# Heads of 64: where the probabilities of an attention are divided by their row sums

## The chip, the cores and the metric

The kernel runs on one core of a Trainium2 chip, in one launch. The metric is the time on the device in microseconds. The kernel before has a median of 2105.86 us over three runs (2103.87 to 2106.68).

## The reference, cut to what matters

A two-layer encoder over 512 positions of width 1024 in float32. Each layer has a feed-forward block, a mixer, a cross-attention to 256 memory positions and a second feed-forward block. In both mixers there are attentions with heads of 64: eight heads in layer 0 (dsa_attention, with a choice of keys by an index), sixteen in layer 1 (chunk_band_attention). All of them end in the same two steps, a softmax over the keys and a product with the values:

```
logits = jnp.einsum('bqhd,bkhd->bhqk', qc, kc).astype(jnp.float32) * dh ** -0.5 + bias[None]
logits = jnp.where(valid, logits, -jnp.inf)
p = jax.nn.softmax(logits, axis=-1).astype(vc.dtype)
return jnp.einsum('bhqk,bkhd->bqhd', p, vc)
```

## The kernel before

TensorE multiplies float32 numbers as pairs of a high and a low part (names that end in h and l: wh and wl, pz0h and pz0l). So one product is three matmuls, and each operand needs a cast on ScalarE (the high part) and a subtraction on VectorE or GpSimd (the low part, such as wl of a weight, L159).

The heads of 64 are computed by attend64, six calls with two passes over j each: four passes in layer 0 ("A" heads), eight in layer 1 ("C" heads). A pass takes a pair of heads, z=0 and z=1. Its steps, in the order in which TensorE does them:

- make_q and make_k turn the queries and keys (L745 and L764: four transposes each), and VectorE and ScalarE split them in two parts (qz, kz);
- close finishes the head z=1 of the pass before;
- the logits of z=0 (L791), then those of z=1. Queries lie on the partitions. A block of 128 queries has its own tile of 128 to 512 keys, e0 to e3. VectorE adds the bias and takes the row maximum in one operation (L804), ScalarE takes the exponential and adds up the row sums rs (L805);
- finish for z=0: ten transposes of 128x128 (L816, transpose_p) bring the keys to the partitions, in the order of e0, e1, e2, e3, and then the further blocks of e1, e2 and e3; ScalarE and VectorE split them (pz0h, pz0l and so on, L819 and L820); eight matmuls (L843) give the output, with queries along the row. The sum of its two parts (L847 on ScalarE, L848 on VectorE) goes to the rows of this head in the pair's tile o (its name in rows is x);
- finish for z=1 is left to the next pass (self.pend).

The output is divided by the row sums only at the end of a pair. rc holds the reciprocals, one column for each block (L869). GpSimd spreads a column over 64 columns (rb, L835), TensorE transposes rb in four pieces (L852), and VectorE multiplies o with the result (L853).

On TensorE the program order is the order written down. Between the steps of the attention stand pieces of a projection, six matmuls of 512 columns each, which weave (L79) pulls: an attention yields a number (its pace), and weave takes pieces, each worth 1300, until the number is used up. So a pace of 600 gives one piece, 1950 two, 2600 two, 3250 three, 4550 four and 0 none. In A the four paces are 3900, 600, 1950 and 0 (after make_k, after the logits of either head, after the transposes, after the PV product); in C they were 4550, 600, 2600 and 600. The orders of VectorE, ScalarE, GpSimd and the DMA queue are set by a scheduler.

In the last passes of A and C the woven pieces belong to the projection of the memory's keys and values (L1083; its tiles are ml, wl, vp and the row sums ss) and to the output projection (L636, whose results are added at L649).

Of the kernel before, what the change touches and what calls it, by code (L numbers as in the profile page):

```python
# [11 lines left out]
F32 = mybir.dt.float32  # L12
# [3 lines left out]
OP = mybir.AluOpType  # L16
# [3 lines left out]
P = 128  # L20
S = 512
# [4 lines left out]
QB = S // P  # L26
# [8 lines left out]

A_QK = 3900
A_S = 600
A_PT = 1950
A_PV = 0
B_QK = 7800  # L40
B_S = 2000
B_PT = 2600
B_PV = 600
C_QK = 4550
C_S = 600
C_PT = 2600
C_PV = 600
I_1 = 1500
# [58 lines left out]
class Encoder:  # L107
# [722 lines left out]
    def attend64(self, qk, vp, vbase, base, gcol, biasname, o_tiles, mp, masks=None):  # L830

        nc = self.nc

        def finish(es, rc, h, z, o, rb):
            nc.gpsimd.tensor_copy(rb.rearrange("p (i c) -> p i c", c=P)[:, :, z * 64:z * 64 + 64],  # L835
                                  rc.unsqueeze(2).to_broadcast([P, QB, 64]))
            self.transpose_p(es)
            yield self.pace[2]
            p = self.bank("pb")
            c = 0  # L840
            for jb, pz, src, q0, n in self.PV:
                for t in self.pz[pz]:
                    nc.tensor.matmul(p[:, q0:q0 + n], vp[jb][:, h * P:(h + 1) * P], t[:, src:src + n],  # L843
                                     start=c == 0, stop=c == 7)
                    c += 1
            tmp = mp.tile([64, S], F32, name="ot", tag="ot", bufs=1)
            nc.scalar.copy(tmp, p[64:128, :])  # L847
            nc.vector.tensor_add(o[z * 64:z * 64 + 64, :], p[0:64, :], tmp)  # L848
            if z == 1:
                p = self.bank("pb")  # L850
                for i in range(QB):
                    nc.tensor.transpose(p[:, i * P:(i + 1) * P], rb[:, i * P:(i + 1) * P], self.ident)  # L852
                nc.vector.tensor_mul(o, o, p)  # L853
                self.done(o)
            yield self.pace[3]

        for j in (0, 1):
            q = self.make_q(qk, j * P)
            k = self.make_k(qk, 256 + j * P, gcol)
            yield self.pace[0]  # L860
            yield from self.close()
            rb = mp.tile([P, S], F32, name="rb", tag="rb", bufs=1)
            sts = []
            for z in (0, 1):
                h = 2 * (base + j) + z
                bias = self.bias_tile(biasname, h, mp)
                es, rs = self.softmax_exp(self.logits(q, k, z, masks), bias, mp)
                rc = self.small.tile([P, 4], F32, name="rc", tag="rc", bufs=4)
                nc.vector.reciprocal(rc, rs)  # L869
                sts.append(finish(es, rc, h - vbase, z, o_tiles[j], rb))  # L870
                yield self.pace[1]
            yield from sts[0]
            self.pend = sts[1]

# [458 lines left out]
    def mixer0(self):  # L1333
        pre, I = "l0_", self.I
        with ExitStack() as ctx:
            self.qkbufs, self.vbufs, self.ebufs = 10, 8, 2
            mp = self.open_mixer(ctx, pre)
            xs, acc = self.xs, self.acc
            os = self.park_x()
            w = I[pre + "w_in"]  # L1340
            nlam = self.lam()
            ga = self.gain_col(pre + "a_q_norm", pre + "a_k_norm", 64 ** -0.5)
            gb = self.gain_col(pre + "b_q_norm", pre + "b_k_norm", 64 ** -0.5)
            sub = self.small.tile([P, 1], F32, name="subg", tag="gcol", bufs=6)
            self.nc.vector.tensor_scalar(sub, self.col(pre + "b_subln"), 1.0 - LAMBDA_INIT, None, op0=OP.mult)
            ready = []
            self.pace = (A_QK, A_S, A_PT, A_PV)

            def gemm():
                self.wshare = WS[0]  # L1350
                ik, iq = [], []
                yield from self.index_gemm(ik, I["l0_w_ikw"], 72, xs)
                for j in range(4):
                    b = []
                    yield from self.index_gemm(b, I["l0_w_iq"][j], P, xs)
                    iq += self.raw(b, mp)
                    if j == 0:
                        v, r = self.var_rstd(acc)
                        ready.append((iq, ik[0], v, r))
                b = []  # L1360
                yield from self.gemm_nat(b, w[0], xs, WS[1])
                bqk = self.heads(b, v, mp)
                b = []
                yield from self.gemm_nat(b, w[1], xs, WS[2])
                bv = self.values(b, r, P, mp)
                ready.append((bqk, bv))
                b = []
                yield from self.gemm_nat(b, w[2], xs, WS[3])
                bqk = self.heads(b, v, mp)
                ready.append((bqk, bv))  # L1370
                b = []
                yield from self.gemm_nat(b, w[3], xs, WS[4])
                aqk = self.heads(b, v, mp)
                b = []
                yield from self.gemm_nat(b, w[4], xs, WS[5])
                av = self.values(b, r, 64, mp)
                ready.append((aqk, av))
                b = []
                yield from self.gemm_nat(b, w[5], xs, WS[6])
                aqk = self.heads(b, v, mp)  # L1380
                ready.append((aqk, av))
                self.wshare = WS[7]
                yield from self.mem_kv(pre, mp)
                yield from self.mix_out(I[pre + "w_out"], list(range(KB)), os, mp)

            def att():
                sc, ik = {}, []
                yield from self.wait(ready, 0)
                iq, p, v, r = ready[0]
                yield from self.index_keys(ik, p, v, r, mp)  # L1390
                yield from self.index_scores(sc, iq, *ik, mp)
                masks = {}
                top = self.index_top(masks, sc, mp)
                yield from self.along(self.wait(ready, 1), top, 1)
                yield from self.along(iter(B_N1), top, TOP_A)
                yield from self.along(self.attend_diff(*ready[1], 0, gb, "bias0", os[0:2], nlam, sub, mp), top, TOP_A)
                yield from self.wait(ready, 2)
                yield B_N2
                yield from self.along(self.attend_diff(*ready[2], 2, gb, "bias0", os[2:4], nlam, sub, mp), top, TOP_B)
                for _ in top:  # L1400
                    pass
                yield from self.wait(ready, 3)
                yield from self.attend64(*ready[3], 0, 0, ga, "bias0", os[4:6], mp, masks)
                yield from self.wait(ready, 4)
                yield from self.attend64(*ready[4], 0, 2, ga, "bias0", os[6:8], mp, masks)
                yield from self.unfinished()

            self.weave(gemm(), att())
            self.xattn(pre, mp)

    def mixer1(self):
        pre, I = "l1_", self.I
        with ExitStack() as ctx:
            self.qkbufs, self.vbufs, self.ebufs = 10, 8, 2
            mp = self.open_mixer(ctx, pre)
# [2 lines left out]
            w = I[pre + "w_in"]  # L1418
            g = self.gain_col(pre + "c_q_norm", pre + "c_k_norm", 64 ** -0.5)
            ready = []  # L1420
            self.pace = (C_QK, C_S, C_PT, C_PV)

            def gemm():
                v = None
# [134 lines left out]
```

## Time and profile before

| what | before |
|---|---|
| median of the runs | 2105.86 us |
| the profiled execution | 2105.58 us |
| its span, first to last instruction | 2103.8 us |
| TensorE busy | 2076.7 us (99%) |
| VectorE busy | 1567.4 us (75%) |
| ScalarE busy | 1135.7 us (54%) |
| GpSimd busy | 363.3 us (17%) |
| granted clock of TensorE | 1.00 throughout |

Busy shares are averages over the whole span. What a step of the attention is worth has to be read in its own stretch: the A pairs lie from about 560 to 655 us, the C pairs from about 1465 to 1680 us. The chain of work that ended last is followed back from the last instruction; where it runs through TensorE without a break, every microsecond on TensorE is one of the kernel.

### The profile page before, as it was taken

The page shows a single profiled execution, that of the slowest core. Times are in us where ns is not written, and L with a number is a line of the kernel's source. Part 1 is how long each engine was busy: PE and PEld are TensorE (multiplying, and loading weights), DVE is VectorE, ACT ScalarE, POOL GpSimd, SP SyncE. Part 2 cuts the span into 40 slices and gives each one's busy share as a digit, 9 for nine tenths or more (in the row PEclk, how much of TensorE's full clock was granted, in tenths as well). Part 3 has the DMA queues.
Part 4 walks back from the last instruction along what each step waited for, and adds up shares of the span by engine and source line. Part 5 has one row for each costly group of instructions (what it writes and reads, how often), then busy time and mean ns, then how long its engine had stood idle before and what let it go on. Part 6 is the DMA issues. An engine that isn't in the chain of part 4 may idle for free.

```text
span 2103.8 us, 32523 instructions
## 1 busy us (share of the span) xinstructions
PE 2076.7 (99%) x12834; PEld 1851.0 (88%) x12834; DVE 1567.4 (75%) x2246; ACT 1135.7 (54%) x1701; POOL 363.3 (17%) x319
## 2 busy tenths in 40 slices
PE   8999999999999999999999999999999999999999
PEld 7989897888788889998989899988888888989997
DVE  8858677699677697685889677684668688958676
ACT  6635344556685565362556254344778566626442
POOL 1101003345421210000020000013453022000000
PEclk9999999999999999999999999999999999999999
DMA  7737535222232176473356366344224225737632
GB/s 225 210 116 193 143 103 162 96 86 80 91 126 69 52 208 165 139 190 116 102 167 182 118 178 174 98 123 150 91 81 131 91 71 150 192 110 190 161 98 93
DMA packets 86122, 279.65 MB, mean 133 GB/s; under 512 B 9681, under 2 KB 12881, under 8 KB 85969
## 3 DMA queue, kind: packets, MB, share of 16 engines
q1 hardware_dynamic: 74448, 235.62, 34.1%
q0 software_dynamic: 11520, 41.95, 11.4%
q8 instruction: 101, 1.65, 0.3%
q14 instruction: 53, 0.43, 0.1%
HBM read 271.24 MB, written 6.29 MB: 132 GB/s over the span
## 4 chain that ended last, share of the span: by engine, by line
PE 87%; DVE 8%; ACT 2%; issue 2%; POOL 1%; DMA 1%; SPq 0%; DVEq 0%; ACTq 0%; POOLq 0%
PE ps_pa L447 26%; PE ps_pb L447 10%; PE ps_pa L583 10%; PE ps_pa L685 10%; PE ps_pb L583 10%; PE ps_pa L636 4%; PE ps_pa L319 3%; PE ps_pb L791 2%; PE ps_pa L1233 1%; PE ps_pb L843 1%; PE ps_pa L1083 1%; PE ps_pb L816 1%; PE ps_pb L636 1%; DVE wl L159 1%; PE ps_pa L1002 1%
## 5 line engine op out<-in xcount | busy, mean ns | idle before, releaser
L157 ACT ACTIVATE wh<-wf 128x1024 fp32r<-128x1024 f32 (+2 forms) x211 | 215.4, 1022 | 347.9 <-PE ps_pa L583 121.0
L159 DVE TENSOR_TENSOR wl<-wf,wh 128x1024 fp32r<-128x1024 f32 (+2 forms) x169 | 199.7, 1185 | 33.4 <-ACT wh L157 31.2
L425 ACT ACTIVATE wh<-s 128x1024 fp32r<-128x1024 f32 x108 | 114.4, 1059 | 105.5 <-PE ps_pb L447 35.0
L426 DVE TENSOR_TENSOR wl<-s,wh 128x1024 fp32r<-128x1024 f32 x108 | 132.5, 1227 | 51.3 <-ACT wh L425 51.1
L425 ACT ACTIVATE wh<-wf 128x1024 fp32r<-128x1024 f32 x84 | 88.9, 1058 | 110.2 <-PE ps_pa L447 36.7
L504 POOL DMA_DIRECT2D s<-l_ffn_wq x40 | 35.5, 887 | 525.8 <-ACT s L503 525.8
L159 POOL TENSOR_TENSOR wl<-wf,wh 128x1024 fp32r<-128x1024 f32 x42 | 101.4, 2415 | 138.1 <-ACT wh L157 136.2
L685 PE MATMUL ps_pa<-wh,xh 128*128 128x512 f32 x384 | 122.0, 399 | 0.1
L685 PE MATMUL ps_pa<-wh,xl 128*128 128x512 f32 x384 | 119.0, 391 | 0.0
L685 PE MATMUL ps_pa<-wl,xh 128*128 128x512 f32 x384 | 118.6, 390 | 0.0
L477 POOL DMA_DIRECT2D s<-l_ffn_wq x40 | 35.6, 889 | 456.6 <-DMA s<-l_ffn_wq 321.4
L426 DVE TENSOR_TENSOR wl<-wf,wh 128x1024 fp32r<-128x1024 f32 x84 | 102.5, 1220 | 8.8 <-ACT wh L425 5.9
L593 DVE TENSOR_TENSOR dn<-ps_pa,R 128x512 f32<-128x512 f32 x48 | 33.1, 689 | 89.2 <-PE ps_pa L583 88.9
L224 POOL TENSOR_TENSOR acc<-acc,sq 128x512 f32<-128x512 f32 (+1 forms) x37 | 54.1, 1462 | 246.4 <-ACT sq L223 245.2
L583 PE MATMUL ps_pb<-hh,wl 128*128 128x512 f32 x352 | 96.2, 392 | 0.0
L583 PE MATMUL ps_pb<-hh,wh 128*128 128x512 f32 x352 | 96.2, 391 | 0.0
L583 PE MATMUL ps_pb<-hl,wh 128*128 128x512 f32 x352 | 96.1, 391 | 0.0
L583 PE MATMUL ps_pa<-hh,wl 128*128 128x512 f32 x328 | 89.4, 392 | 0.0
L583 PE MATMUL ps_pa<-hl,wh 128*128 128x512 f32 x328 | 89.3, 391 | 0.0
L583 PE MATMUL ps_pa<-hh,wh 128*128 128x512 f32 x328 | 89.3, 391 | 0.0
L593 DVE TENSOR_TENSOR dn<-ps_pb,R 128x512 f32<-128x512 f32 x48 | 33.0, 688 | 73.4 <-PE ps_pb L583 72.9
L685 PEld LDWEIGHTS ps_pa<-wl,xh 128*128 128x128 f32 x384 | 72.1, 188 | 15.8
(377 smaller groups left out, 5938.4 us busy)
## 6 DMA issues: line engine op xcount, KB each, us to landing
wf<-l_ffn_wq SPq DMA_DIRECT2D x120, 512.0 KB, 3.6
s<-l_ffn_wq SPq DMA_DIRECT2D x80, 512.0 KB, 4.5
s<-l_ffn_wq POOLq DMA_DIRECT2D x80, 512.0 KB, 6.7
wf<-l_ffn_wd SPq DMA_DIRECT2D x64, 512.0 KB, 3.9
wf<-l_w_in SPq DMA_DIRECT2D x48, 512.0 KB, 3.3
wf<-l_ffn_wd SPq DMA_DIRECT2D x32, 384.0 KB, 3.1
wf<-l_mem_wkv SPq DMA_DIRECT2D x16, 512.0 KB, 3.3
wf<-l_w_out SPq DMA_DIRECT2D x16, 512.0 KB, 3.3
```

Source lines behind the costliest of these rows:

```text
L157: self.leading = nc.scalar.activation(wh[:, sl], w[:, sl], AF.Copy)
L159: eng.tensor_sub(wl[:, sl], w[:, sl], wh.bitcast(F32)[:, sl])
L224: self.summed = (eng or nc.gpsimd).tensor_add(acc[:, :n], acc[:, :n], sq[:, :n])
L319: nc.tensor.matmul(p, w[a][:, k * P:(k + 1) * P], xs[k][c], start=k == order[0] and a == c == 0, stop=k == order[-1] and a == 1)
L425: self.leading = nc.scalar.activation(h, t, AF.Copy)
L426: self.parted = nc.vector.tensor_sub(l, t, h.bitcast(F32))
L447: self.nc.tensor.matmul(bank[:, sl], w[a][:, o:o + P], xs[k][b], start=first and z == a == b == k == 0, stop=z == a == 1 and k == KB // 2 - 1,
L583: self.nc.tensor.matmul(bank, w[a][:, j * P:(j + 1) * P], h, start=j == a == e == 0, stop=j == nb - 1 and (a, e) == ops[-1])
L593: nc.vector.tensor_mul(t, bank, f.R)
L636: nc.tensor.matmul(banks[dd], a[:, o:o + P], parts(k)[b], start=k == first and a is wh and b == 0, stop=k == last and a is wl)
L685: nc.tensor.matmul(banks[i], xs[k][a][:, i * P:(i + 1) * P], w[b][:, kk * 512:kk * 512 + 512], start=k == a == b == 0, stop=k == KB - 1 an ...
L791: nc.tensor.matmul(bank[:, o:o + n], a, b[:, :n], start=c == 0, stop=c == len(ops) - 1)
```

## The change

It divides the probabilities instead of the outputs. For each block of queries VectorE now takes the reciprocal of the row sums (128x1) and multiplies the block's tile e in place, before the transposes: 96 reciprocals and 96 scalings, 24 each of 128, 256, 384 and 512 columns. The tile rb, its copies on GpSimd, its transposes and the last multiplication are gone. The pace after the logits now may differ between the two heads: in C the one after make_k falls from 4550 to 3250 and the one after the logits of z=1 rises from 600 to 1950; in A both stay.

```
-C_QK = 4550
+C_QK = 3250
 C_S = 600
+C_SS = 1950
...
-        def finish(es, rc, h, z, o, rb):
-            nc.gpsimd.tensor_copy(rb.rearrange("p (i c) -> p i c", c=P)[:, :, z * 64:z * 64 + 64],
-                                  rc.unsqueeze(2).to_broadcast([P, QB, 64]))
+        def finish(es, h, z, o):
             self.transpose_p(es)
...
             if z == 1:
-                p = self.bank("pb")
-                for i in range(QB):
-                    nc.tensor.transpose(p[:, i * P:(i + 1) * P], rb[:, i * P:(i + 1) * P], self.ident)
-                nc.vector.tensor_mul(o, o, p)
                 self.done(o)
             yield self.pace[3]
...
-            rb = mp.tile([P, S], F32, name="rb", tag="rb", bufs=1)
...
                 rc = self.small.tile([P, 4], F32, name="rc", tag="rc", bufs=4)
-                nc.vector.reciprocal(rc, rs)
-                sts.append(finish(es, rc, h - vbase, z, o_tiles[j], rb))
-                yield self.pace[1]
+                for i in range(QB):
+                    nc.vector.reciprocal(rc[:, i:i + 1], rs[:, i:i + 1])
+                    nc.vector.tensor_scalar(es[i], es[i], rc[:, i:i + 1], None, op0=OP.mult)
+                sts.append(finish(es, h - vbase, z, o_tiles[j]))
+                yield self.pace[1][z]
...
-            self.pace = (C_QK, C_S, C_PT, C_PV)
+            self.pace = (C_QK, (C_S, C_SS), C_PT, C_PV)
```

TensorE, fourth C pair, where the PV product of the head z=1 of the third pair ends (L843) and the logits of z=0 (L791) follow; before:

```order
L843 MATMUL ps_pb<-pz2h,vp 128x256
L843 MATMUL ps_pb<-pz2l,vp 128x256
L852 MATMUL ps_pb<-ident,rb 128x128 x4
L685 MATMUL ps_pa<-wh,xh 128x512 x2
L685 MATMUL ps_pa<-wh,xl 128x512 x2
L685 MATMUL ps_pa<-wl,xh 128x512 x2
L791 MATMUL ps_pb<-kz0h,qz_14184 128x256
L791 MATMUL ps_pb<-kz0l,qz_14184 128x256
```

and in the changed kernel (its line numbers differ a little):

```order
L845 MATMUL ps_pb<-pz2h,vp 128x256
L845 MATMUL ps_pb<-pz2l,vp 128x256
L687 MATMUL ps_pa<-wh,xh 128x512 x2
L687 MATMUL ps_pa<-wh,xl 128x512 x2
L687 MATMUL ps_pa<-wl,xh 128x512 x2
L793 MATMUL ps_pb<-kz0h,qz_14204 128x256
L793 MATMUL ps_pb<-kz0l,qz_14204 128x256
```

Only the four transposes of rb are gone; the woven piece of six matmuls stays. In A no piece stands there. Next, TensorE in the same pair, from the end of the logits of z=1 to the transposes of z=0; before:

```order
L791 MATMUL ps_pb<-kz1h,qz_14185 128x512
L791 MATMUL ps_pb<-kz1l,qz_14185 128x512
L685 MATMUL ps_pa<-wh,xh 128x512 x2
L685 MATMUL ps_pa<-wh,xl 128x512 x2
L685 MATMUL ps_pa<-wl,xh 128x512 x2
L816 MATMUL ps_pb<-ident,e_15426 128x128
L816 MATMUL ps_pb<-ident,e_15429 128x128
L816 MATMUL ps_pb<-ident,e_15432 128x128
L816 MATMUL ps_pb<-ident,e_15435 128x128
```

and in the changed kernel:

```order
L793 MATMUL ps_pb<-kz1h,qz_14205 128x512
L793 MATMUL ps_pb<-kz1l,qz_14205 128x512
L687 MATMUL ps_pa<-wh,xh 128x512 x2
L687 MATMUL ps_pa<-wh,xl 128x512 x2
L687 MATMUL ps_pa<-wl,xh 128x512 x2
L687 MATMUL ps_pa<-wh,xh 128x512 x2
L687 MATMUL ps_pa<-wh,xl 128x512 x2
L687 MATMUL ps_pa<-wl,xh 128x512 x2
L818 MATMUL ps_pb<-ident,e_15448 128x128
L818 MATMUL ps_pb<-ident,e_15451 128x128
L818 MATMUL ps_pb<-ident,e_15454 128x128
L818 MATMUL ps_pb<-ident,e_15457 128x128
```

Two pieces stand there instead of one; the second comes from the four between make_k and close. The fourth transpose reads the longest tile, e3. The last place is VectorE in the third A pair, from the maxima of z=1 on (ISA rows, the second of each two stores the maximum); before:

```order
L804 ISA e_6276,m<-ps_pb,bias 128x128
L804 ISA m 128x1
L804 ISA e_6279,m<-ps_pb,bias 128x256
L804 ISA m 128x1
L869 RECIPROCAL rc<-rs 128x4
L804 ISA e_6282,m<-ps_pb,bias 128x384
L804 ISA m 128x1
L804 ISA e_6285,m<-ps_pb,bias 128x512
L804 ISA m 128x1
L649 TENSOR_TENSOR x<-ps_pa,xr 128x512 x2
```

and in the changed kernel, where e_6252 and e_6255 are the tiles e2 and e3 of z=0, and e_6292 to e_6301 those of z=1:

```order
L806 ISA e_6292,m<-ps_pb,bias 128x128
L806 ISA m 128x1
L806 ISA e_6295,m<-ps_pb,bias 128x256
L806 ISA m 128x1
L865 RECIPROCAL rc<-rs 128x1
L866 TENSOR_SCALAR e_6252<-e_6252,rc 128x384
L806 ISA e_6298,m<-ps_pb,bias 128x384
L806 ISA m 128x1
L806 ISA e_6301,m<-ps_pb,bias 128x512
L806 ISA m 128x1
L866 TENSOR_SCALAR e_6255<-e_6255,rc 128x512
L865 RECIPROCAL rc<-rs 128x1
```

The scaling of e3 of z=0 stands behind all four maxima of z=1. It does so in each of the twelve pairs, and in the pairs C6 and C7 of layer 1 a wl (L161) and, in C7, a vp (L1093) and a row sum (L698) stand ahead of it as well.

## Rows read from the trace of the kernel before

**Rows 1.** Page: busy time by engine; chain that ended last, by engine.

```profile
PE 2076.7 (99%) x12834; PEld 1851.0 (88%) x12834; DVE 1567.4 (75%) x2246; ACT 1135.7 (54%) x1701; POOL 363.3 (17%) x319
...
PE 87%; DVE 8%; ACT 2%; issue 2%; POOL 1%; DMA 1%; SPq 0%; DVEq 0%; ACTq 0%; POOLq 0%
```

**Rows 2.** Waits of TensorE: total us, times, longest us.

```profile
PE ps_pb L816 <- DVE qz L755: 2.5, 2, 2.1
```

**Rows 3.** Chain that ended last, pair C3: start us, length us, what.

```profile
1520.39 0.44 PE ps_pb L852 x4
1520.82 1.39 PE ps_pa L685 x6
...
1527.56 1.09 PE ps_pb L816 x10
```

**Rows 4.** Lines L852 and L853: ns of one, min/median/max; first and last start.

```profile
L852 PE MATMUL ps_pb<-ident,rb x48: 270/272/273, 590.3 to 1672.7; 128*128 128x128 f32 x48
...
L853 DVE TENSOR_TENSOR x<-x,ps_pb x12: 679/686/689, 592.4 to 1674.0; 128x512 f32<-128x512 f32 x12
```

**Rows 5.** Line L970, a scaling elsewhere in the kernel: ns of one.

```profile
L970 DVE TENSOR_SCALAR sc<-rl,coef x3: 353/420/485, 385.5 to 386.5; 128x256 f32<-128x256 f32 x1, 128x384 f32<-128x384 f32 x1, 128x512 f32<-128x512 f32 x1
```

**Rows 6.** Timeline of VectorE in C3, end of the maxima of z=1: start, us.

```profile
1526.53 0.17 DVE L869 RECIPROCAL rc<-rs 128x4 f32<-128x4 f32 x1
1526.62 0.66 DVE L804 CUSTOM_DVE_ANT_0 e<-ps_pb,bias 128x512 f32<-128x512 f32 x1
1527.21 0.08 DVE L804 DVE_READ_ACCUMULATOR2_ANT m<- 128x1 f32 x1
```

**Rows 7.** Chain that ended last, pairs A2 and A3.

```profile
597.45 1.09 PE ps_pb L816 x10
...
607.60 1.15 PE ps_pb L816 x10
...
623.67 1.29 PE ps_pb L843 x8
```

**Rows 8.** Timeline of VectorE in A2 (first two rows) and A3.

```profile
591.12 0.68 DVE L848 TENSOR_TENSOR x<-ps_pb,ot 64x512 f32<-64x512 f32 x1 [1.08 <-ACT ot L847]
...
596.70 0.09 DVE L804 DVE_READ_ACCUMULATOR2_ANT m<- 128x1 f32 x1
...
622.57 0.55 DVE L820 TENSOR_TENSOR pz2l<-ps_pb,pz2h 128x384 fp32r<-128x384 f32 x1
```

**Rows 9.** Timelines of VectorE (two rows) and GpSimd in A1.

```profile
571.05 0.49 DVE L1079 SCALAR_TENSOR_TENSOR ml<-mem,cols,mh 128x256 fp32r<-128x256 f32 x1 [0.54 <-ACT mh L1077]
...
573.17 0.08 DVE L804 DVE_READ_ACCUMULATOR2_ANT m<- 128x1 f32 x1
...
573.40 2.39 POOL L159 TENSOR_TENSOR wl<-wf,wh 128x1024 fp32r<-128x1024 f32 x1
```

**Rows 10.** Timelines of GpSimd and VectorE at three places in layer 1.

```profile
1494.65 1.64 POOL L244 TENSOR_TENSOR f<-ss,mhalf 128x8 f32<-128x8 f32 x1
1495.19 0.23 DVE L699 TENSOR_SCALAR ss<-ss,epsv 128x8 f32<-128x8 f32 x1
...
1531.85 2.40 POOL L159 TENSOR_TENSOR wl<-wf,wh 128x1024 fp32r<-128x1024 f32 x1
1532.80 1.48 DVE L699 TENSOR_SCALAR ss<-ss,epsv 128x8 f32<-128x8 f32 x1
...
1577.76 2.41 POOL L159 TENSOR_TENSOR wl<-wf,wh 128x1024 fp32r<-128x1024 f32 x1 [5.72 <-ACT wh L157]
1579.27 1.44 DVE L1308 TENSOR_TENSOR ol<-x,oh 128x512 fp32r<-128x512 f32 x1
```

**Rows 11.** Two stretches: length; busy us of PE, PEld, DVE, ACT, POOL; clock.

```profile
1465.00:1600.00 135.00, 134.39 (x716) 114.78 (x715) 88.06 (x195) 99.05 (x206) 58.00 (x51) 1.00 0.26 84
1602.80:1637.00 34.20, 33.46 (x178) 27.51 (x177) 31.52 (x72) 29.65 (x64) 9.14 (x14) 1.00 0.49 159
```

More of the change, by code (lines that the diff above doesn't have):

```diff
@@ L37 @@
 A_S = 600
+A_SS = 600
 A_PT = 1950
@@ L1346, in mixer0 @@
             ready = []
-            self.pace = (A_QK, A_S, A_PT, A_PV)
+            self.pace = (A_QK, (A_S, A_SS), A_PT, A_PV)
             def gemm():
```

## Prediction

> **What bounds the kernel now.** I read the page first. TensorE is busy 2076.7 us of the 2103.8 us span and the chain that ended last runs through it for 87%; VectorE comes second with 1567.4 us [rows 1]. Then the waits of TensorE: over the whole program its longest in the attention is 2.5 us in two pieces, at the transposes of the probabilities [rows 2]. So around the change TensorE has next to no slack: work taken off it counts in full, and so does each new wait of it. The question is whether VectorE, which gets the new work, delivers in time.
>
> I call the four pairs of heads of layer 0 A1 to A4 and the eight of layer 1 C1 to C8; each is one pass of the loop over j, with the heads z=0 and z=1.
>
> **What is removed.** Twelve groups of four transposes. A group is one piece of 0.44 us of the chain [rows 3]; its line has 48 of 272 ns each [rows 4], which overlap, so the chain's piece is the price: 12 x 0.44 = 5.3 us. With them go 12 products of 0.69 us on VectorE [rows 4] and the copies on GpSimd, which is busy for 17% [rows 1].
>
> **What is added.** Per head four scalings in place, of 128, 256, 384 and 512 columns. The nearest row (L970) has 0.35, 0.42 and 0.485 us for 256, 384 and 512 columns [rows 5]; the step of 0.07 puts 128 columns at 0.29. On VectorE an operation starts some 0.08 us before the one ahead ends: the reciprocal of 128x4 lasts 0.17 and the next starts 0.09 after it [rows 6]. So the four take about 0.21 + 0.27 + 0.34 + 0.40 = 1.2 us, the removed product 0.6. The three further reciprocals take 0.09 each (one of a single column has no row: between 0.03 and 0.09). A head costs VectorE some 1.5 us more, a pair 2 x 1.5 - 0.6 = 2.4 us more.
>
> **What is moved.** In each C pair a piece of six matmuls, 1.39 us [rows 3], goes from ahead of the z=1 transposes of the pair before (C1: from ahead of the logits of z=0) to behind the logits of z=1. It costs nothing by itself, since TensorE runs the same pieces, and gives the probabilities of z=0 1.39 us more before their transposes. Those of z=1 lose as much and keep some 10 us (in A2 the transposes of z=0 start at 597.45, those of z=1 at 607.60 [rows 7]): nothing. In A nothing moves.
>
> **Where VectorE is late.** The order of instructions puts the scaling of the longest block of z=0 (e3) behind the four maximum operations of z=1 in every pair. These wait for the logits of z=1, and the fourth of the ten transposes needs e3. The ten take 1.09 us [rows 7], so the fourth starts 0.33 us into them (3 of 10).
>
> *A2 to A4*, by A2: TensorE loses 0.44 us, so the transposes of z=0 would start at 597.45 - 0.44 = 597.01 and need e3 at 597.34. VectorE began the addition of L848 at 591.12 and ended the last maximum of z=1 at 596.79, with little idle time between [rows 8]. It sheds 0.60 there (the product) and gets three scalings (0.82) and 0.27 of reciprocals, then the scaling of e3 (0.48): 597.76. TensorE waits 0.4 us in each of the three, 0 to 0.7. In A3 more comes: pz2l ended at 623.12 [rows 8], 1.35 us ahead of its first reader, the sixth of the eight matmuls that start at 623.67 [rows 7]. All the additions of the pair, some 2.3 us, now stand ahead of it: 0.6, 0 to 1.0.
>
> *A1* has no pair ahead, so nothing is shed. The last maximum ended at 573.25; with 1.1 us more, of which 0.54 fills idle time [rows 9], and the scaling, e3 is ready at 574.3, 0.2 us late by the same reckoning. But GpSimd runs L159 from 573.40 to 575.79 there [rows 9], and that operation has held VectorE: L699, 0.23 us at 1495.19, took 1.48 us from 1532.80 to 1534.28 while GpSimd ran L159 until 1534.25, and ol took 1.44 us under another L159 [rows 10]. Held so, e3 comes 1.7 us late. Between 0.2 and 1.8 I take 1.2, since by the rows GpSimd starts first.
>
> *C1 to C4*, by C3: the transposes of z=0 now start at 1527.56 - 0.44 + 1.39 = 1528.51 [rows 3] and need e3 at 1528.84. The last maximum of z=1 ended at 1527.29 [rows 6]; logits come 0.44 earlier, 1.1 us are added ahead of it and the scaling behind it: 1528.4. So 0.4 us are spare: no wait, 0.1 each for the spread, 0 to 0.3. *C5* has an L159 of GpSimd over its scalings [rows 10]: 0.4, 0 to 1.1. *C8* has a further wl ahead of e3: 0.3, 0 to 0.6.
>
> *C6 and C7* lie where the keys and values of the memory are projected, and there VectorE is nearly full: 31.52 us busy of the 34.20 from 1602.80 to 1637.00 [rows 11]. They bring 2.4 us (C6) and 0.9 (C7 up to its e3): 34.8 us of work in a stretch that TensorE would now do in 34.2 - 0.9 = 33.3. The excess is 1.5 us if VectorE never idles and 4.2 if it keeps its 2.7 us of idle time. In C7 the scaling of e3 also stands behind a wl, a vp and a row sum. I take 3.0.
>
> **The sum**: -5.3 + 1.2 (A1) + 1.2 (A2 to A4) + 0.6 (pz2l in A3) + 0.4 (C1 to C4) + 0.4 (C5) + 3.0 (C6, C7) + 0.3 (C8) = +1.8 us. The profiled execution took 2105.58 us (1.78 outside its span); the median of the runs, 2105.86, is 0.3 above it. From the profiled one: 2107.4 us. With all lower ends it is -5.3 + 1.7 = -3.6, or 2102.0; with all upper ends -5.3 + 1.8 + 2.1 + 1.0 + 1.2 + 1.1 + 4.2 + 0.6 = +6.7, or 2112.3. A change of under 0.2% (4.2 us) can hardly be told from none in this kernel, and most of this lies within it.
>
> **Rivals.** *All of it hides* (0.24). VectorE is idle for a quarter of the span, the first additions of a pair may find idle time that I counted as busy, and ScalarE may deliver its exponentials earlier. Then the 5.3 us remain: 2100.3. For it, the waits of all twelve pairs must stay under 1.1 us together; the 92% of C6 and C7 [rows 11] speak against it.
>
> *GpSimd holds the scalings* (0.18; this one ends slower). In C GpSimd is busy 58 of 135 us [rows 11]. If in each of C1 to C5 one scaling of z=0 is held over an L244 of 1.64 us [rows 10], 1.24 remain after what is spare: 5 x 1.24 - 0.8 (counted above) + 0.6 (A1 at its upper end) = +6.0 on the forecast, 2113.4 us. It decides from about 2.9 us upwards, two to three pairs held. Against it: L699 took its 0.23 us at 1495.19 in the middle of an L244 [rows 10]. The Trainium skill (SBUF — State Buffer, section Who interferes with whom) states that such a VectorE operation and any GpSimd operation exclude each other for the whole instruction, whoever starts first. By that rule L244 holds too; the rows on L159 agree with it and the one on L244 does not, if only for eight columns.
>
> *VectorE saturates* (0.14): in C6 and C7 each wait of TensorE also delays what VectorE prepares for the woven pieces, and the two cost 6 us or more instead of 3.0: 2110.4 and up.
>
> That the transposes remain is excluded by the order of instructions.
>
> **How the numbers follow.** The forecast has 0.44, and most of it lies from 2103 to 2111. Faster by over 0.2% needs waits of under 1.1 us in all: the first rival, 0.24. Slower by over 0.2% needs over 9.5 us of them: nearly all of the second rival, most of the third and the upper end of the forecast, together 0.30. No change to be told has the rest, 0.46. The range goes from the first rival to the second, 2100 to 2113; the forecast's own is 2102 to 2112.
>
> **What would show it.** After the change, L852 and L835 are gone and TensorE is busy about 5 us less. TensorE waits for the scaling (L866) at the transposes (L818) some 2 to 3 us in A and 1 to 4 us in C6 and C7, and not in C1, C3 and C4. The scalings of 512 columns take 0.49 us, with a few of over 1.5 us while GpSimd runs L161. I am wrong if those transposes wait over 0.5 us in each of C1 to C4, if C6 and C7 cost under 1 us, or if scalings are held under L244 (L246 then).

## The result, and the profile after

The changed kernel takes 2121.47 us (median of six runs, 2116.42 to 2122.77) against 2105.62 us before: 1.0072 times as long, 95% interval 1.0061 to 1.0082. It is 15.9 us slower; the forecast was +1.8, and the time lies 8.5 us beyond the range of 2100 to 2113.

The page of the changed kernel, busy time and chain, as in [rows 1]:

```profile
PE 2079.6 (98%) x12782; PEld 1850.1 (87%) x12786; DVE 1597.5 (75%) x2402; ACT 1137.5 (54%) x1701; POOL 355.7 (17%) x295
...
PE 84%; DVE 11%; ACT 2%; issue 2%; DMA 1%; POOL 0%; SPq 0%; DVEq 0%; ACTq 0%; POOLq 0%
```

The span is 2120.1 us, 16.3 more. TensorE does fewer instructions and is yet busy 2.9 us longer, and VectorE's part of the chain has grown from 8% to 11%. VectorE's 30 us more are about what was expected (12 x 2.4 = 29). The waits of TensorE, where [rows 2] had 2.5 us as the most in the attention (total us, times, longest):

```profile
PE ps_pb L818 <- DVE e L866: 7.2, 9, 2.1
PE ps_pa L638 <- DVE vp L1093: 2.6, 1, 2.6
PE ps_pb L818 <- DVE qz L757: 2.5, 2, 2.1
PE ps_pb L843 <- DVE pz2l L822: 1.9, 1, 1.9
```

The first row is the wait that the prediction was about: 7.2 us at the transposes, for the scaling. The second is a wait for vp, which the moved piece brings and not the scalings (e1 and e2 below have 2.15 us of it without any). The fourth is one for pz2l, which stood behind a scaling. The third was there before the change. The places, from TensorE's own timeline (in brackets the idle time just before, and who ended it):

```profile
577.69 0.98 PE L818 MATMUL ps_pb<-ident,e 128*128 128x128 f32 x7 [2.08 <-DVE e L866]
601.14 0.98 PE L818 MATMUL ps_pb<-ident,e 128*128 128x128 f32 x7 [0.26 <-DVE e L866]
623.72 0.98 PE L818 MATMUL ps_pb<-ident,e 128*128 128x128 f32 x7 [0.31 <-DVE e L866]
630.25 0.39 PE L843 MATMUL ps_pb<-pz2l,vp 128*128 128x256 f32 x1 [1.88 <-DVE pz2l L822]
649.64 0.98 PE L818 MATMUL ps_pb<-ident,e 128*128 128x128 f32 x7 [0.30 <-DVE e L866]
...
1512.23 0.98 PE L818 MATMUL ps_pb<-ident,e 128*128 128x128 f32 x7 [0.85 <-DVE e L866]
...
1593.09 0.98 PE L818 MATMUL ps_pb<-ident,e 128*128 128x128 f32 x7 [0.82 <-DVE e L866]
1621.71 0.98 PE L818 MATMUL ps_pb<-ident,e 128*128 128x128 f32 x7 [1.50 <-DVE e L866]
1649.11 0.76 PE L638 MATMUL ps_pa<-oh,wh 128*128 128x512 f32 x1 [2.56 <-DVE vp L1093]
1677.69 0.98 PE L818 MATMUL ps_pb<-ident,e 128*128 128x128 f32 x7 [0.61 <-DVE e L866]
```

Seven of the ten transposes wait each time, from the one that needs e3 on. The places are A1, A2, A3 (twice), A4, C2, C5, C6, C7 and C8. C1, C3 and C4 do not wait, as forecast. The new idle time of TensorE adds up to 13.6 us over the whole trace (35.8 against 22.2 us, gaps of over 0.08 us; 0.6 of it ahead of the first matmul), and 13.6 - 5.3 would leave only 8.3 of the 16.3. Laid beside the trace before, the same matmul starts 0.2 us earlier at 550 us, 7.7 us later at 664 and 16.3 us later at 1705: about half of the loss lies at the A pairs, in which nothing was moved (with the first of the three stretches below).

A second thing has changed: the granted clock, which was 1.00 throughout before and is 0.998 on the mean now. Four stretches around the wait for pz2l in A3 show it (length; busy us of PE, PEld, DVE, ACT, POOL; then the clock):

```profile
624.00:628.00 4.00, 4.00 (x23) 3.44 (x22) 4.00 (x12) 2.53 (x6) 1.06 (x2) 1.00 0.63 197
628.00:630.50 2.50, 0.62 (x5) 0.35 (x4) 2.50 (x3) 0.00 (x0) 1.45 (x1) 1.00 0.42 105
631.00:635.00 4.00, 4.00 (x16) 3.23 (x15) 2.80 (x4) 3.72 (x7) 0.00 (x0) 0.59 0.56 197
635.00:639.00 4.00, 4.00 (x24) 3.45 (x23) 1.38 (x2) 2.31 (x4) 0.00 (x0) 0.98 0.01 4
```

TensorE stands idle for 1.88 us. In the 4 us shown behind it TensorE has a full load of work at a mean clock of 0.59: it runs at half clock, 1.2 instead of 2.4 GHz, for some 3.4 us, does 16 matmuls against 24 in the next 4 us, and loses 1.7 us on top of the wait. There are three such stretches in this trace, at 549.8, 631.7 and 1648.9: up to 5.1 us. The first follows a wait of 2.06 us, the longest of [rows 2], that was there before the change too, in code ahead of the A pairs that did not change, and then without a fall of the clock. With 13.6 + 5.1 - 5.3 = 13.4 us, 2.9 of the 16.3 remain, in small steps that I did not attribute.

### The profile page after: what moved, and what is told of

Its sections match the earlier page's. It is cut to its first block, busy times and chain, and to the rows that moved or that the text cites. A ratio compares the mean times of both kernels' runs of the same rounds, so it can differ in the third digit from the quotient of the medians.

```text
span 2120.1 us, 32521 instructions
## 1 busy us (share of the span) xinstructions
PE 2079.6 (98%) x12782; PEld 1850.1 (87%) x12786; DVE 1597.5 (75%) x2402; ACT 1137.5 (54%) x1701; POOL 355.7 (17%) x295
## 4 chain that ended last, share of the span: by engine, by line
PE 84%; DVE 11%; ACT 2%; issue 2%; DMA 1%; POOL 0%; SPq 0%; DVEq 0%; ACTq 0%; POOLq 0%
PE ps_pa L449 25%; PE ps_pb L449 10%; PE ps_pa L585 10%; PE ps_pb L585 10%; PE ps_pa L687 9%; PE ps_pa L638 4%; PE ps_pa L321 3%; PE ps_pb L793 2%; PE ps_pa L1230 1%; PE ps_pb L843 1%; DVE wl L161 1%; PE ps_pb L638 1%; PE ps_pb L818 1%; PE ps_pa L999 1%; PE ps_pa L1080 1%
## 5 line engine op out<-in xcount | busy, mean ns | idle before, releaser
L161 DVE TENSOR_TENSOR wl<-wf,wh 128x1024 fp32r<-128x1024 f32 (+2 forms) x169 | 199.5, 1184 | 37.7 <-ACT wh L159 35.5
L161 POOL TENSOR_TENSOR wl<-wf,wh 128x1024 fp32r<-128x1024 f32 x42 | 101.9, 2427 | 165.5 <-ACT wh L159 163.7
L687 PEld LDWEIGHTS ps_pa<-wl,xh 128*128 128x128 f32 x384 | 72.5, 189 | 15.9
```

The costliest lines, as they stand in the source:

```text
L161: eng.tensor_sub(wl[:, sl], w[:, sl], wh.bitcast(F32)[:, sl])
L687: nc.tensor.matmul(banks[i], xs[k][a][:, i * P:(i + 1) * P], w[b][:, kk * 512:kk * 512 + 512], start=k == a == b == 0, stop=k == KB - 1 an ...
```

## The experiments

The runs beside which each was timed gave 2105.8 to 2106.4 us for the kernel before. Lines are shown against the changed kernel unless said otherwise.

**The two halves of the change apart.** The "moved pause" is the moved piece of the prediction: a place where the attention pauses for a piece of a projection. e1 leaves out the division altogether, with the paces of the change; e8 also puts the paces of before back, so that only the removal is left; e2 is the kernel before with the moved pause alone.

e1 and e8:

```
-                for i in range(QB):
-                    nc.vector.reciprocal(rc[:, i:i + 1], rs[:, i:i + 1])
-                    nc.vector.tensor_scalar(es[i], es[i], rc[:, i:i + 1], None, op0=OP.mult)
```

e8 also:

```
-C_QK = 3250
+C_QK = 4550
 C_S = 600
-C_SS = 1950
+C_SS = 600
```

e2, against the kernel before:

```
-C_QK = 4550
+C_QK = 3250
 C_S = 600
+C_SS = 1950
...
-                yield self.pace[1]
+                yield self.pace[1][z]
...
-            self.pace = (C_QK, C_S, C_PT, C_PV)
+            self.pace = (C_QK, (C_S, C_SS), C_PT, C_PV)
```

> The changed kernel with neither the 96 reciprocals nor the 96 scalings; the division by the row sums is left out. Theory (VectorE is late with the scalings, and nothing else of the change costs): the waits that the change brought vanish and the removal alone remains, 12 x 0.44 = 5.3 us, so 2100.3 us (2098 to 2102), no new stretch at half clock in the attentions. Rival (the removal or the moved pieces cost something themselves, for instance by shifting the phase of the pieces woven in): above 2105 us.

> The kernel before with only the moved pause: in C one piece goes from ahead of the z=1 transposes to behind the logits of z=1; division of the outputs as before. Theory: no more than 1 us either way, 2104.6 to 2106.6, since TensorE does the same work and waits for nothing new. Rival (the moved piece takes cover from the z=1 head or from the query and key splits): over 2108 us, with new waits of TensorE in C1 to C8.

> The changed kernel without reciprocals and scalings (the division is left out) and with the paces of before. If removal and moved pause add up (e1 2105.35 with both, e2 2111.38 with the pause alone, so 5.5 us for the pause and 6.0 for the removal), this gives 2099.9 us (2099 to 2101). Rival (the removal is worth little by itself and e2 was slow for another reason): 2103 to 2106 us.

e8 took 2100.82 us, 0.9976 (0.9967 to 0.9986) of before: the removal is worth 5.1 us, as priced. e2 took 2111.38 us, 1.0025 (1.0016 to 1.0034): the moved pause, priced at nothing, costs 5.5 us. e1 took 2105.35, no different from before (0.9988 to 1.0006): the two cancel. For e1 and e2 the theory missed and the rival hit; for e8 the theory hit. The reciprocals and scalings then cost 2121.5 - 2105.4 = 16.1 us on top of e1.

Where the pause costs is seen in C7 of e2, in the timelines of VectorE (two rows) and TensorE.

```profile
1636.13 1.50 DVE L160 TENSOR_TENSOR wl<-wf,wh 128x1024 fp32r<-128x1024 f32 x1
1637.56 0.74 DVE L1097 SCALAR_TENSOR_TENSOR vp<-ps_pa,mem_r,vp 128x512 fp32r<-128x512 f32 x1
...
1638.45 0.47 PE L637 MATMUL ps_pa<-oh,wh 128*128 128x512 f32 x1 [2.15 <-DVE rc L870]
```

The piece that now comes later relative to the heads is the last of the memory's projection. Its result is taken out of its bank (a part of ps_pa, which TensorE writes and VectorE reads) by vp. That operation used to be done ahead of the maxima of z=1; now it stands behind them and a wl, ends at 1638.30, and the first piece of the output projection needs that bank at 1636.30. (The row blames the reciprocal of L870, which ends with vp; at the same place the changed kernel's row names vp, with 2.56 us.) The wait of 0.25 us that was there before has become 2.15; 0.87 us come in C5, at the PV product for pz0l, and 0.33 and 0.48 in C6. Between 1465 and 1700 us TensorE waits 4.6 us in e2 and 1.3 before: 3.3 of the 5.5 us. e1, with the same paces and no scaling at all, has the same long wait in C7 and also 4.6 us in all:

```profile
PE ps_pa L638 <- DVE vp L1089: 2.2, 1, 2.2
```

The other 2.2 us of the pause are not shown. They are not a stretch at half clock behind the long wait, as far as was seen: the profiled executions of e1 (2104.84 us) and e2 (2109.69) have none there.

**The paces of before with the scalings.** e3 has the two constants of e8 and the scalings.

> The changed kernel with the paces of before (one piece behind the logits of z=1 instead of two). Theory: the transposes of z=0 come 1.39 us earlier in each C pair and VectorE is no sooner done, so C1, C3 and C4, which did not wait, now wait about 1 us each and C2 and C5 to C8 up to 1.4 us more: 5 to 10 us slower than the changed kernel, 2126 to 2131 us, perhaps a further 1.7 us for each wait that brings a stretch at half clock. Rival (the paces do not matter, the scalings are late by far more than a piece or not at all): within 2 us of the changed kernel.

It took 2122.82 us, within 2 us of the changed kernel, so by the number its rival hit; but not for its reason. The waits for the scaling rose by 4.2 us (total us, times, longest):

```profile
PE ps_pb L818 <- DVE e L866: 11.4, 11, 2.6
```

while the waits of the moved pause went (0.26 instead of 2.56 us for vp in C7, none for pz0l). C3 now waited 1.16 us, as foreseen; C1 and C4 did not wait. So beside the scalings the pause takes about as much as it gives.

**Which engine.** e4 puts the scalings on ScalarE.

```
-                    nc.vector.tensor_scalar(es[i], es[i], rc[:, i:i + 1], None, op0=OP.mult)
+                    nc.scalar.activation(es[i], es[i], AF.Copy, scale=rc[:, i:i + 1])
```

> The changed kernel with the 96 scalings on ScalarE instead of VectorE (the reciprocals stay on VectorE). Theory (it is the place in VectorE's queue and the holding by GpSimd that make the scalings late): ScalarE works 0.4 to 0.7 us for each, is half idle, and is not held; the waits shrink to those of C6 and C7, where ScalarE has 29.7 of 34.2 us already: 2101 to 2110 us. Rival (the extra step between exponential and transpose is late on any engine, since the exponentials themselves end late): 2115 us or more, with the waits at the same transposes.

It took 2132.77 us, 11 more than on VectorE; the theory missed and the rival hit by its number. The waits for the scaling, and then the line itself (ns min/median/max):

```profile
PE ps_pb L818 <- ACT e L866: 15.2, 11, 2.9
```

```profile
L866 ACT ACTIVATE e<-e,rc x96: 385/550/739, 572.3 to 1691.1; 128x128 f32<-128x128 f32 x24, 128x256 f32<-128x256 f32 x24, 128x384 f32<-128x384 f32 x24, 128x512 f32<-128x512 f32 x24
```

ScalarE is idle for nearly half the span, but its exponentials stand in the queue just there and each now has a scaling beside it. A low mean share says little of the stretch in which an engine is needed.

**GpSimd's holding.** In A1 and A3 of the changed kernel a scaling of VectorE begins while GpSimd runs a woven weight's low part (L161), and takes some 2 us: it is held. In C2 one begins while GpSimd runs L246:

```profile
574.91 2.35 POOL L161 TENSOR_TENSOR wl<-wf,wh 128x1024 fp32r<-128x1024 f32 x1
575.81 2.28 DVE L866 TENSOR_SCALAR e<-e,rc 128x512 f32<-128x512 f32 x3
...
627.08 2.37 POOL L161 TENSOR_TENSOR wl<-wf,wh 128x1024 fp32r<-128x1024 f32 x1 [0.90 <-ACT wh L159]
627.46 2.27 DVE L866 TENSOR_SCALAR e<-e,rc 128x512 f32<-128x512 f32 x1
629.65 0.55 DVE L822 TENSOR_TENSOR pz2l<-ps_pb,pz2h 128x384 fp32r<-128x384 f32 x1
...
1511.94 1.73 POOL L246 TENSOR_TENSOR f<-ss,mhalf 128x8 f32<-128x8 f32 x1
1513.07 0.49 DVE L866 TENSOR_SCALAR e<-e,rc 128x512 f32<-128x512 f32 x1
...
1589.29 2.73 POOL L161 TENSOR_TENSOR wl<-wf,wh 128x1024 fp32r<-128x1024 f32 x1 [8.34 <-ACT wh L159]
1590.84 1.74 DVE L1305 TENSOR_TENSOR ol<-x,oh 128x512 fp32r<-128x512 f32 x1
...
1592.57 0.46 DVE L866 TENSOR_SCALAR e<-e,rc 128x512 f32<-128x512 f32 x1
```

The row at 575.81 joins three scalings, of which the first took 1.83 us. Behind the one at 627.46 stands pz2l, for which TensorE waits in A3. The last three rows are from C5: there not the scaling was held but the ol ahead of it, 1.74 us instead of 0.69.

Of the 96 scalings of this trace 69 began while GpSimd was idle and took 0.26 to 0.49 us. Five began under L161: 0.77 to 2.27 us, each ending some 0.1 to 0.4 us after it. Thirteen began under L246: 0.28 to 0.49 us, not held. Of three under the products of L705 two were held (0.59 and 1.07). Six under a memset (L829) were not. e5 takes L161 off GpSimd in these attentions.

```
+        self.in64 = False
...
-            eng = nc.gpsimd if self.wshare and self.wcount % self.wshare == 0 else nc.vector
+            eng = nc.gpsimd if self.wshare and self.wcount % self.wshare == 0 and not self.in64 else nc.vector
...
+        self.in64 = True
         def finish(es, h, z, o):
...
-            self.attending = False
+            self.attending = self.in64 = False
```

> The changed kernel with the low parts of the woven weights (L161) on VectorE throughout the attentions of heads of 64; GpSimd has 13 fewer of 2.4 us, VectorE 13 more of 1.2 us. Theory (a large share of the waits is the holding of VectorE by those operations: A1 2.1, pz2l in A3 1.9 with its stretch at half clock, C2 1.2, C5 0.8): the scalings of 128x512 all take 0.49 us, A1 waits under 0.6 and A3 under 0.5, and the time falls to 2112 to 2118 us in spite of the load. Rival (VectorE is simply full): not under 2121 us.

2113.56 us: 7.9 us less, although VectorE has 19 operations of 1.2 us more (the expectation had counted 13). The theory hit. Its detail for A3 held (the wait for pz2l and its stretch at half clock are gone), that for A1 did not: A1 still waits 2.36 us for e3, since a wl of VectorE now stands ahead of that scaling:

```profile
570.76 1.21 DVE L162 TENSOR_TENSOR wl<-wf,wh 128x1024 fp32r<-128x1024 f32 x1
...
571.98 0.46 DVE L868 TENSOR_SCALAR e<-e,rc 128x512 f32<-128x512 f32 x1
```

**The order on VectorE.** e6 makes the two longest maxima of z=1 follow the scaling of e3 of z=0.

```
-    def softmax_exp(self, lg, bias, mp):
+    def softmax_exp(self, lg, bias, mp, after=None):
...
+            with self.behind(after if i >= 2 else None):
                 self.mark = nc.vector.tensor_tensor_reduce(e, bank[:, o:o + n], ...
...
+            scaled = None
...
-                    nc.vector.tensor_scalar(es[i], es[i], rc[:, i:i + 1], None, op0=OP.mult)
+                    scaled = nc.vector.tensor_scalar(es[i], es[i], rc[:, i:i + 1], None, op0=OP.mult)
```

> The changed kernel with one thing more: the maxima of the two longest blocks of z=1 are issued on VectorE behind the scaling of e3 of z=0 (before, all four stood ahead of it). Theory (the order in VectorE's queue makes e3 late): the waits of 0.3 us in A2 to A4 vanish, those of C5, C6 and C8 at these transposes fall by 0.6 to 1.2 each: 2115 to 2119 us. Rival (e3 waits for its exponential or for GpSimd anyway): within 1.5 us of 2121.5.

2114.23 us, 7.2 less, a little more than expected (2115 to 2119). The waits for the scaling fell from 7.2 to 2.2 us; that of A1 is gone, though L161 is on GpSimd as before:

```profile
PE ps_pb L819 <- DVE e L868: 2.2, 4, 0.9
```

e7 adds two things: the scalings of z=1 are issued only behind pz2l of z=0, and the paces are those of before. (scale is the loop of reciprocals and scalings; self.mark is pz2l here.)

```
+            if z == 0:
+                with self.behind(self.mark):
+                    scale(*later)
...
+                if z == 0:
+                    scaled = scale(es, rs)
+                else:
+                    later = (es, rs)
```

> The order of e6, the scalings of z=1 issued behind the three subtractions pz0l to pz2l of z=0, and the paces of before. Theory (order and moved pause are the larger part of the loss; holding by GpSimd stays): pause -5.5, order and late scalings -4 to -8 with the stretch at half clock in A3: 2106 to 2113 us. Rival (with the paces of before e3 of z=0 is late in every C pair whatever the order, as in e3, 2122.8): 2117 us or more.

2107.06 us (ratio to before 0.9998 to 1.0015): the theory hit. Against e3, which has the same paces, order and late scalings together are worth 15.8 us, nearly the whole of the 16.1, with all the scalings still on VectorE and L161 still on GpSimd. So it is the place of the scalings in the queue that costs, not their time.

**What a wait costs.** The kernel before with idle row sums on VectorE ahead of pz2l of z=0 in A1 to A4, four in e9, seven in e10 and e13. e9 and e10 write them to a new tile of 4 bytes, e13 to one that was there. e14 has the new tile without the sums, with one memset of it for each call.

e13, against the kernel before:

```
+            if t == 2:
+                for _ in range(self.delay):
+                    with self.behind(self.mark):
+                        scrap = self.small.tile([P, 4], F32, name="scrap", tag="es0")
+                        self.mark = nc.vector.tensor_reduce(scrap[:, 0:1], self.pz[0][1].bitcast(F32), axis=AX, op=OP.add)
...
+            self.delay = 7 if masks is not None and z == 0 else 0
```

The new tile of e9, e10 and e14:

```
+        scrap = self.small.tile([P, 1], F32, name="scrap", tag="scrap", bufs=2)
```

> The kernel before with four idle row sums of 0.61 us on VectorE ahead of pz2l of z=0 in A1 to A4, which make TensorE wait in the PV product by 4 x 0.61 less the 0.75 to 1.5 us to spare there: 1.0, 1.7, 1.1 and 1.2, together 4.9 us. Theory (a wait costs itself, and a further 1.7 us only where a stretch at half clock follows, which came behind waits of 1.9 us and more): 2110 to 2112 us, at most one new stretch at half clock, in A2. Rival (half clock comes by chance, or with any wait): several stretches also here, 2113 us or more.

> As e9 with seven row sums: waits of about 2.8, 3.5, 2.9 and 3.0 us, 12.2 together. Theory: each of the four waits is followed by a stretch at half clock of some 3.4 us, which costs 1.7: 12.2 + 6.8 = 19.0, so 2125 us (2121 to 2127), clock 0.997 or less. Rival (the clock does not answer to these waits): 2118 us, clock as before.

> e10 (the kernel before with seven idle row sums ahead of pz2l in A1 to A4), with the sums written to a tile that was there already, so that no address in the on-chip memory moves. Theory (the drift of e9 and e10 in the feed-forward blocks is the moved addresses): the 512-column matmuls go back to 391 to 392 ns, and only the waits remain: idle time about 16 us more, four to six stretches of 3.4 us at half clock at 1.7 each: 2128 to 2133 us. Rival (the waits slow the later matmuls): 2145 us again.

> The kernel before with the further small tile of e9 and e10 and one memset of it for each call, no waits. Theory (addresses): 2118 to 2122 us, the 512-column matmuls at 394 to 395 ns. Rival: within 1 us of before.

e9 took 2132.75 us and e10 2147.2: both far over the theory, e10 also far over its rival, and mostly for a reason that has nothing to do with waits (so e9, above its rival's 2113 us, does not bear the rival out). e14, without any wait, took 2121.87 us; e13, with seven sums and no new tile, 2130.78. In both the theory hit. So some 16 us of e9 and e10 are the tile. A line of a feed-forward block shows it, first in the kernel before, then in e14 (busy us, mean ns):

```profile
L583 PE MATMUL ps_pb<-hh,wl 128*128 128x512 f32 x352 | 96.2, 392 | 0.0
```

```profile
L583 PE MATMUL ps_pb<-hh,wl 128*128 128x512 f32 x352 | 97.3, 394 | 0.0
```

e13 is the clean one. Its waits, in A1 to A4:

```profile
PE ps_pb L852 <- DVE pz2l L827: 16.7, 4, 6.5
```

That is 16.7 us, 4.5 more than I had worked out from the spare times (A2's alone is 6.5), yet the kernel is 25 us slower. The trace has five stretches at half clock, each beside a wait of over 2 us; four are 3.4 us long and one 6.8. The first, behind the wait at 546 to 550 us, has nothing to do with the sums. The other four are 17.1 us long, but 4.4 of them fall into the waits themselves, when TensorE has nothing to do; the remaining 12.7 cost half, 6.3 us. 16.7 + 6.3 = 23.0, and the A pairs take 23.8 us more than in the trace before.

Over all 18 profiles I counted the waits of TensorE of over 1.2 us, without the one ahead of its first matmul. A stretch at half clock began in the wait or behind it in 1 of 16 cases under 1.5 us, in 15 of 34 from 1.5 to 2.3 us, and in 15 of 16 over 2.3 us. In the middle it goes either way for the same wait: the one of 2.06 us at 546 to 550, ahead of the attentions and the same in 13 of these traces, had it in 8 of them.

**Toward a better version.** e11 is e7 with L161 on VectorE as in e5; e12 is e6 with the paces of before and L161 on VectorE; e15 is e11 with the moved pause in the pairs C5 and C6 only; e16 is e15 with the scalings of z=1 on GpSimd.

e15, against e11:

```
+                    d = 1300 if n == 2 else 0
+                    self.pace = (C_QK - d, (C_S, C_SS + d), C_PT, C_PV)
```

e16, against e15:

```
-                    scale(*later)
+                    scale(*later, nc.gpsimd)
```

> e7 (order, late scalings of z=1, paces of before; 2107.1 us) and the low parts of the woven weights on VectorE as in e5, so that GpSimd holds no scaling for 2.4 us. Theory (holding is what is left of the loss beside C6 and C7): the scalings held in e7 (2.55 us each at 1481 and 1556, 1.63 at 625) are free, against VectorE's further 13 x 1.2 us: 2101 to 2106 us. Rival (what is left is VectorE's load, which this raises): 2107 us or more.

> e6 (order alone) with the paces of before and the low parts of the woven weights on VectorE; the scalings of z=1 stand where the scheduler puts them. Theory: as e11, less what the late scalings were worth; without holding they were worth little, so within 2 us of e11: 2101 to 2107 us. Rival (the scalings of z=1 ahead of pz0l to pz2l cost by themselves): 3 us or more above e11.

> e11 (2105.75 us) with the moved pause in the pairs C5 and C6 only, where e11 waits 1.57 us for e3 of C6; C7 keeps the paces of before, so that its vp is not late. Theory: the wait in C6 falls under 0.4 us and nothing is put in its place: 2104.4 us (2103.5 to 2105). Rival (C6 is late by VectorE's load and the moved piece does not help, or C7 is later for it): 2105.5 us or more.

> e15 with the scalings of z=1 on GpSimd, which has no woven weights there and 10 us for them. Theory (the waits left in A2, 1.8 us for the splits of keys, and in C7, 1.0, are VectorE's load): VectorE has 1.2 us less for each pair, both fall by 0.5 to 1.2 us: 2102 to 2104 us. Rival (GpSimd's scalings hold VectorE's operations with two inputs, and last about 1 us each for 512 columns): 2105 us or more.

e11 took 2105.75 us, as its theory had it, and e12 2108.48: without holding, late scalings are still worth 2.7 us, so neither e12's theory nor its rival quite hit. e15 took 2104.74 us (0.9987 to 1.0005 of before), as expected, though its C6 still waits 0.72 of the 1.57 us. e16 took 2114.3, and its rival hit by the number: in A4 and C8, the last pair of either layer, the head z=1 is not left for a next pass, and GpSimd's scalings, 4.3 us for the four in A4, come too late for its transposes.

```profile
PE ps_pb L820 <- POOL e L843: 4.3, 5, 1.2
```

No version that divides is measurably faster than the kernel before. e15 keeps about 1 of the 5.1 us of the removal by its median, which lies within the noise.

## Why the prediction was wrong

Right: what bounds the kernel; the removal (5.3 forecast, 5.1 in e8); VectorE's added time; the waits of A2 to A4 for e3 (0.4 each forecast; 0.26, 0.31 and 0.30); C1, C3 and C4 without a wait; e3 of z=0 late because of its place in VectorE's queue (e6). None of the three signs of being wrong that it named came: of C1 to C4 only C2 waited over 0.5 us, C6 cost 1.5, and nothing was held under L246. They were all signs about the waits for the scaling, and what was missing lay elsewhere. Only "TensorE is busy about 5 us less" gave it away: it was busy 2.9 us more.

Wrong, by the steps of the prediction:

| term | forecast us | in the trace after, us |
|---|---|---|
| the moved pause | 0 | 0.88 in C5, 0.32 in C6, 2.56 in C7; alone 5.5 by e2 |
| A1 | 1.2 | 2.08 |
| A2 to A4 | 1.2 | 0.87 |
| A3, pz2l | 0.6 | 1.88 |
| C1 to C4 | 0.4 | 0.40 + 0.85, both in C2 |
| C5 | 0.4 | 0.82 |
| C6 and C7 | 3.0 | 1.50 in C6, none for a scaling in C7 |
| C8 | 0.3 | 0.61 |
| clock | none | 3 x 1.7: ahead of A, in A3, in C7 |

*"It costs nothing by itself, since TensorE runs the same pieces"* is the first step that failed. TensorE's work is the same, but a woven piece has a result that VectorE takes out, and in C7 that operation fell behind the maxima. I had priced what the heads gain by the moved piece, not what is late for the piece. By itself the pause costs 5.5 us (e2).

*"each new wait of it counts in full"* is the second: a long one counts for more. The prediction has no term for the clock. The changed kernel loses up to 5.1 us to it in the profiled run, 1.7 of them by chance, beside the wait at 546 to 550 us that the change does not touch. The spread of its runs fits as well: one with a mean clock of 0.999 took 2116.42 us, those with 0.996 to 0.998 took 2119.70 to 2122.77.

The third is what GpSimd holds. I counted it in A1, as 0.2 to 1.8 us, where the wait was 2.08, and nowhere else in A; but L161 also ran over the longest scaling of z=1 in A3, which then held up pz2l. A1 itself is not settled by holding: its wait goes with the order of e6, L161 staying where it was, and stays without L161 on GpSimd in e5. In the rival the holding stood for C1 to C5, with L246; there the holding under L246 did not happen (13 of 13 not held), and C2 was held by L705. The 0.82 us of C5 came near the forecast by a held ol, not by a held scaling. The Trainium skill (SBUF — State Buffer, Who interferes with whom) has such a VectorE operation excluded by any GpSimd operation. L161 and two of three L705 agree, L246 and the memsets of L829 do not. By e5, L161 costs the changed kernel 7.9 us net, with what follows from it in the clock. That gain and the 7.2 us of e6 nearly add up, to 15.1: e12 has both, at the paces of before, and lies 14.3 us under e3. Behind the late scalings of e7 little of it is left: e11 gains 1.3 us, within the noise.

The waits that the forecast had a term for came to 9.0 us where it had 7.1. The larger part of the miss of 14 us are the two terms that it lacked, the pause (5.5 alone) and the clock (up to 5.1); they cannot simply be added, since beside the scalings the pause also gives cover (e3). Left open: the 2.9 us of the span that neither the idle time nor the clock explains, 2.2 us of the pause alone, and why L246 does not hold.

## What to carry to other kernels

When work moves from an engine that is always busy to one that is busy for three quarters, price its place in the queue, not its time: here 5.1 us were gained on TensorE and 16 lost by some 30 us of work on VectorE that stood at the wrong places, of which another order of two operations gave nearly half back (e6), and later scalings with the old paces nearly all (e7). When a piece of filler work is moved, follow its result to the operation that empties its bank. And count a wait of the matrix engine of about 2 us, as they were here, at up to twice its length, since a stretch at half clock that costs 1.7 us often followed.

## What was not expected of the hardware

In or behind waits of TensorE of over 2.3 us the granted clock fell to half in 15 of 16 cases, mostly for 3.4 us, in three cases for 6.8 or 10.2 us, of which a part lay in the wait; for the one of 2.06 us it fell in 8 of 13 traces of nearly the same program.

One further tile of 4 bytes a partition lengthened the 512-column matmuls of the feed-forward blocks from 391 and 392 ns to 394 and 395 and the kernel by 16 us (e14). The way is not shown: it may move what is laid behind it in the on-chip memory, but the traces list no addresses. It is the tile and not the operation on it, since e9 and e10 have it without e14's memset and e13 has their sums without it. Between the starts of those matmuls lay 232.4 ns in e9, e10 and e14 against 228.9 before, which for 2040 of them is 7.1 us; the 6720 matmuls of 256 columns of the same blocks take 12.4 us more from start to start in e14, waits included, and other places a little less. Of two versions that differ in their tiles, this has to be taken out before anything else is compared, as e13 does. The changed kernel has lost a tile too (rb), but there the 512-column matmuls lie 229.1 ns apart and the two kinds together take 0.7 us more: its 16 us lie elsewhere.
